# Attention results kept transposed through the out-projection of a hybrid encoder layer

## The chip, the cores and the metric

The kernel runs on one core of a Trainium2 chip. Its engines work side by side, each through a queue of its own in order: TensorE (PE, the matrix multiplier; PEld is its weight load), VectorE (DVE), ScalarE (ACT), GpSimd (POOL) and SyncE (SP), which issues nearly all DMAs. The metric is the device time of one execution in microseconds; lower is better.

## What is computed

One encoder layer on x of 1024 tokens by 1024 features, float32, cut here to what the change touches:

```python
hn = rms_norm(x, norm1_g); proj = hn @ w_in          # qa ka va | qb kb vb
out_a = global_gqa_attention(qa, ka, va)             # dense softmax, 8 heads of 64, 2 kv heads
out_b = dilated_mixture_attention(qb, kb, vb)        # 3 dilated windows, 8 heads of 64, merged
mixed = concatenate([rms_norm(out_a, outa_norm_g),   # each over its own 512 features
                     rms_norm(out_b, outb_norm_g)], -1)
x = x + mixed @ w_out
x = x + conv_ffn(rms_norm(x, norm2_g), ...)          # up, depthwise conv, gelu gate, down
```

Each attention result is a sum over keys divided by a softmax denominator; the two RMS norms follow, one scale per token and half.

## The kernel before

The kernel is one stream of Python calls; a scheduler puts each engine's instructions in order from them by its own estimates, and waits are semaphores between the queues. A few instructions are pinned behind another (`tc.issue_after`). Large products run in fp32 split into a high and a low part, three 128x512 matmuls for each product (xh wh, xh wl, xl wh). The stages follow one another: in-projection, dense attention, dilated attention, out-projection, feed-forward.

`qab(t)` is the mix: eight tiles of 128 tokens by 1024 features, the left 512 columns from the dense heads, the right 512 from the dilated ones.

Dense attention has 16 groups g, each one block of 128 queries and one of two kv heads (4 query heads). The scores of eight key tiles come in four pairs (L763, L764), ACT takes the exponential and the high part (L773), DVE the low part (L774), and pv (L747) gathers 66 rows in a PSUM bank: 64 features and the denominator, by 4 x 128 queries. `last` copies the bank to the single buffer F_OT (DVE, L757). One group later `o_turn` has PE transpose it in four pieces (L752), and `o_norm` takes the reciprocal of the denominators (L793) and multiplies it into the mix (L794).

Dilated attention has 8 heads of 4 iterations, n = 4h + i: scores (L976), exponential on ACT (L977), weights from a table on DVE (L985; or L989, L991, L992 for the iterations with a high and a low part), and two iterations later the product with the values (L1004, L1011). After the fourth, ACT copies the two banks to F_OS (L1014, L1015), and `b_out` turns them with eight transposes on PE (L1044), again followed by `o_norm`. Loads of the next heads' keys, values and tables run on SP; POOL prepares some operands.

Out-projection: `mix_sq` sums squares on ACT (L1089), `mix_norm` makes the two scales and brings the right half to the scale of the left (L1098), `mix_tr` transposes four 128x128 pieces on PE (L196) and splits them into high and low (ACT L219, DVE L220). `proj_out` (L1116 to L1118) adds up eight blocks k of 128 features in a pair of banks per tile, out of three pairs. `h2_a` scales the sum and adds x (L1127), then norm2 on ACT and DVE (L1130 to L1140); `h2_b` transposes the result (L196 too) for the up-projection (L1567 to L1569). Weights of w_out are loaded and split (`wo_load`, `wo_high`, `wo_low`) late in the dilated loop.

## Time and profile before

| | |
|---|---|
| median of 3 runs | 1187.44 us (1187.07 to 1187.44) |
| the profiled execution | 1187.63 us, its span 1185.8 us |
| PE busy | 1172.6 us, 99% of the span, 5896 matmuls |
| DVE busy | 1009.8 us, 85% |
| ACT busy | 659.9 us, 56% |
| POOL busy | 332.1 us, 28% |
| DMA on the hardware queue | 146.43 MB, 38.5% of sixteen engines' span |

Busy PE means that some matmul is in flight: matmuls are pipelined and overlap, so what one costs is read from the distance between two starts. A group's idle time names what ended the wait before it. In windows, the numbers in brackets count instructions.

### The profile page before, as it was taken

How to read it: one execution, taken by the hardware profiler on the slowest of the kernel's cores; microseconds unless marked ns; L12 is line 12 of the kernel's file. 1: busy time of each engine (PE TensorE's matmuls, PEld its weight loads, DVE VectorE, ACT ScalarE, POOL GpSimd, SP SyncE). 2: the span in 40 equal slices, each digit the busy share in tenths (PEclk: the TensorE clock that was granted, in tenths of full speed). 3: DMA queues.
4: the chain of work that ended last, by engine and by line, in shares of the span. 5: the costliest groups of instructions: out<-in, count | busy, mean ns of one | idle time of the engine just before them, and what ended most of it. 6: DMA issues, size and time to landing. Idle time of an engine off the chain costs nothing.

```text
span 1185.8 us, 16414 instructions
## 1 busy us (share of the span) xinstructions
PE 1172.6 (99%) x5896; PEld 966.2 (81%) x5896; DVE 1009.8 (85%) x1431; ACT 659.9 (56%) x986; POOL 332.1 (28%) x237
## 2 busy tenths in 40 slices
PE   9999999999999999999999999999999999999998
PEld 8888886666679998887888888888888888888886
DVE  7869888899988887668999999999999997966672
ACT  7865638799887876346534443444534463543431
POOL 0000221510034510011556465555556414000000
PEclk9999999999999999999999999999999999999999
DMA  8556230110036555232223323232323358967961
GB/s 319 179 145 162 80 78 1 25 52 1 10 67 142 127 127 195 72 102 67 81 98 101 112 100 123 80 107 98 116 98 104 114 192 300 333 217 235 313 231 67
DMA packets 122839, 153.30 MB, mean 129 GB/s; under 512 B 51072, under 2 KB 78336, under 8 KB 122624
## 3 DMA queue, kind: packets, MB, share of 16 engines
q1 hardware_dynamic: 120608, 146.43, 38.5%
q0 software_dynamic: 2144, 5.77, 2.2%
q8 instruction: 47, 0.77, 0.3%
q14 instruction: 40, 0.33, 0.1%
HBM read 113.64 MB, written 33.82 MB: 124 GB/s over the span
## 4 chain that ended last, share of the span: by engine, by line
PE 90%; DVE 5%; ACT 2%; POOL 1%; DMA 1%; issue 1%; SPq 0%; ACTq 0%; POOLq 0%; DVEq 0%
PE ps L1569 12%; PE ps L1568 12%; PE ps L1567 12%; PE ps L747 6%; PE ps L1709 6%; PE ps L1711 6%; PE ps L1710 6%; PE ps L439 3%; PE ps L440 3%; PE ps L441 3%; PE ps L976 3%; PE ps L1118 2%; PE ps L1116 2%; PE ps L1011 2%; PE ps L1117 2%; PE ps L763 2%
## 5 line engine op out<-in xcount | busy, mean ns | idle before, releaser
L1567 PE MATMUL ps<-bigr 128*128 128x512 f32 x616 | 239.8, 389 | 0.5 <-ACT bigr L1170 0.5
L1568 PE MATMUL ps<-bigr 128*128 128x512 f32 x616 | 239.7, 389 | 0.0
L1569 PE MATMUL ps<-bigr 128*128 128x512 f32 x616 | 239.6, 389 | 0.0
L1606 DVE SCALAR_TENSOR_TENSOR bigf<-bigf 128x768 f32<-128x768 f32 (+1 forms) x176 | 193.3, 1134 | 0.7
L1535 ACT ACTIVATE bigr<-bigf 128x512 fp32r<-128x512 f32 x154 | 91.7, 622 | 140.9 <-POOL bigf L1527 108.9
L1689 ACT ACTIVATE bigr<-bigf 128x1024 fp32r<-128x1024 f32 (+1 forms) x99 | 83.8, 868 | 115.4 <-PE ps L1711 63.2
L1567 PEld LDWEIGHTS ps<-bigr 128*128 128x128 f32 x616 | 115.6, 188 | 25.0 <-ACT bigr L1170 0.9
L1568 PEld LDWEIGHTS ps<-bigr 128*128 128x128 f32 x616 | 115.6, 188 | 23.9
L1569 PEld LDWEIGHTS ps<-bigr 128*128 128x128 f32 x616 | 115.6, 188 | 23.9
L1690 DVE TENSOR_TENSOR bigr<-bigf,bigr 128x1024 fp32r<-128x1024 f32 (+1 forms) x99 | 97.6, 1005 | 27.5 <-ACT bigr L1689 24.2
L1709 PE MATMUL ps<-bigr 128*128 128x512 f32 x308 | 119.8, 389 | 0.0
L1710 PE MATMUL ps<-bigr 128*128 128x512 f32 x308 | 119.8, 389 | 0.0
L1711 PE MATMUL ps<-bigr 128*128 128x512 f32 x308 | 119.8, 389 | 0.0
L1536 DVE TENSOR_TENSOR bigr<-bigf,bigr 128x512 fp32r<-128x512 f32 x112 | 106.0, 949 | 3.1 <-ACT bigr L1535 2.6
L747 PE MATMUL ps<-bigr 128*66 128x512 f32 x384 | 99.9, 394 | 0.0
L439 PE MATMUL ps<-bigr 128*128 128x512 f32 x224 | 87.4, 390 | 0.0
L441 PE MATMUL ps<-bigr 128*128 128x512 f32 x224 | 87.2, 389 | 0.0
L440 PE MATMUL ps<-bigr 128*128 128x512 f32 x224 | 87.2, 389 | 0.0
L774 DVE TENSOR_TENSOR bigr<-bigf,bigr 128x1024 fp32r<-128x1024 f32 x64 | 81.0, 1271 | 5.3 <-ACT bigr L773 4.8
L1572 DVE TENSOR_TENSOR bigf<-ps,bigf 128x512 f32<-128x512 f32 x110 | 75.0, 681 | 5.1 <-PE ps L1569 4.9
L1536 POOL TENSOR_TENSOR bigr<-bigf,bigr 128x512 fp32r<-128x512 f32 x42 | 66.9, 1593 | 33.0 <-ACT bigr L1535 31.9
L747 PEld LDWEIGHTS ps<-bigr 128*66 128x66 f32 x384 | 50.8, 136 | 29.9
(224 smaller groups left out, 2380.7 us busy)
## 6 DMA issues: line engine op xcount, KB each, us to landing
bigf<-w_down SPq DMA_DIRECT2D x99, 256.0 KB, 4.3
bigf<-w_up SPq DMA_DIRECT2D x44, 512.0 KB, 3.6
bigf<-gscr SPq DMA_DIRECT2D x77, 256.0 KB, 4.4
gscr<-bigf SPq DMA_DIRECT2D x31, 512.0 KB, 2.6
bigf<-x SPq DMA_DIRECT2D x16, 512.0 KB, 4.4
bigf<-w_in SPq DMA_DIRECT2D x29, 256.0 KB, 3.1
bigf<-xT SPq DMA_DIRECT2D x16, 256.0 KB, 6.6
bigf<-w_out SPq DMA_DIRECT2D x8, 512.0 KB, 3.5
```

The source lines that it names most:

```text
L439: mm(o, r(a, 128), r(w, 512), start=(k == 0 and n != 2 and (c == 1 or n != 3)), stop=False, skip_group_check=True)
L440: mm(o, r(a, 128), r(w + 512, 512), start=False, stop=False, skip_group_check=True)
L441: mm(o, r(a + 512, 128), r(w, 512), start=False, stop=(k == 3), skip_group_check=True)
L747: mm(bank(ob)[0:66], r(w, 66), r(p + 512 * u, 512), start=(kt == 0 and i == 0), stop=(kt == 7 and i == 2))
L1536: low = lambda eng: eng.tensor_tensor(rp(o + 512, [128, 4], [1, 128]), src, rfp(o, [128, 4], [1, 128]), op=OP.subtract)
L1567: mm(bank(b), wh, th, start=(k == 0 and n in (1, 5, 6, 7)), stop=False, skip_group_check=True)
L1568: mm(bank(b), wh, tl, start=False, stop=False, skip_group_check=True)
L1569: mm(bank(b), wl, th, start=False, stop=(k == 3), skip_group_check=True)
L1606: vec.scalar_tensor_tensor(f(a + o, n), f(i + d, n), w_, f(a + o, n), op0=OP.mult, op1=OP.add)
L1709: mm(o, ah, r(d, 512), start=(q == 0 and n in (1, 5, 2)), stop=False, skip_group_check=True)
L1710: mm(o, ah, r(d + 1024, 512), start=False, stop=False, skip_group_check=True)
L1711: mm(o, al, r(d, 512), start=False, stop=(q == NQ - 1), skip_group_check=True)
```

## The change

The transposes between attention and out-projection are left out. In the new form the mix holds features on partitions and tokens along the free axis: in tile `qab(t)` block k of 128 columns is feature block k of those 128 tokens, which is what the matmuls take as weights.

Dense: `last` issues four DMAs on SP for each group. Two move the 64 feature rows from F_OT into the mix (L763; `qab(b)`, 64 partitions each), two write the denominators to `dna` in DRAM (L765). After eight groups `recip_load` brings 128x32 denominators to the chip, `recip` takes one reciprocal and stores it to `rna`, and `scale_load` spreads a row of it over 64 partitions by DMA. `scale_a` multiplies the mix by it on DVE; `squares` squares on ACT and adds four feature blocks on DVE (a 128x128 sum), and `squares_sum` adds up the partitions by matmuls with a column of ones (128x1). All this is placed in groups 8 to 15 (`dense_late`) and in the dilated loop for the second half (`dilated_late`).

Dilated: values come three iterations after the scores, not two. After a head's last iteration a DMA gathers the denominators into 128x8; one iteration later `b_move` moves the features into the mix, another one later `b_recip` takes the reciprocal, stores it to `rnb` and spreads it over 64 partitions, and `scale_b` multiplies two heads at once.

Out-projection: each tile's sum comes in two parts, u = 0 (dense half, four k) and u = 1 (dilated half), each with the two halves of 512 columns in banks of its own. `part_add` (L1195) scales a part by its own norm and adds x or the sum so far. The sixteen parts run in the order `parts`; `mix_split` (ACT L1200, DVE L1201) splits what `mix_tr` gave before. The Sqrt of the dense half's norm stands behind the dilated loop in the program. Blocks 4 and 5 of w_out are split after the loop. A general branch of the program, for inputs beyond a limit, keeps the old form and is not run here.

```diff
-            def o_turn():
-                t = next_tr()
-                for i in range(4):
-                    nc.tensor.transpose(bank(t, 66, 128 * i), f(F_OT + 128 * i, 128)[0:66], f(O_IDF, 66)[0:66])
-                o_norm(t, 128, qab(b) + 256 * kv, ([64, 4], [1, 64]))
-
             def last():
                 pv(3)
                 vec.tensor_copy(f(F_OT, 512)[0:66], bank(ob)[0:66])
+                for u in range(2):
+                    dma(f(qab(b) + 256 * kv, 256)[64 * u:64 * u + 64].rearrange("p (c n) -> p c n", c=2),
+                        fp(F_OT + 128 * u, [256, 2], [1, 128])[0:64])
+                    dma(dna[u:u + 1, b, 256 * kv:256 * kv + 256].rearrange("o (c n) -> o c n", c=2),
+                        fp(F_OT + 128 * u, [256, 2], [1, 128])[64:65])
 
...
-            behind, turn[:] = turn[:], [o_turn]
-            return [lambda: [t() for t in [lambda: pv(1)] + behind], lambda: pv(2), last, o_turn if g == 15 else None]
+            return [lambda: pv(1), lambda: pv(2), last]
+
+        def recip_load(half):
+            dma(fp(F_RC + 32 * half, [16, 2], [1, 16]), dna[:, 4 * half:4 * half + 4, :].rearrange("u b (p e) -> (b p) u e", e=16))
+
+        def recip(half):
+            vec.reciprocal(f(F_RC + 32 * half, 32), f(F_RC + 32 * half, 32))
+            dma(rna[:, 4 * half:4 * half + 4, :].rearrange("u b (p e) -> (b p) u e", e=16), fp(F_RC + 32 * half, [16, 2], [1, 16]))
+
+        def spread_row(dst, row, n):
+            return bass.AP(tensor=row.tensor, offset=row.offset, ap=[[0, 64], [1, n]])
+
+        def scale_load(t):
+            for u in range(2):
+                dma(rf(R_RBA[t % 3], 512)[64 * u:64 * u + 64], spread_row(None, rna[u, t], 512))
+
+        def scale_a(t):
+            vec.tensor_tensor(f(qab(t), 512), f(qab(t), 512), rf(R_RBA[t % 3], 512), op=OP.mult)
+
+        def squares(t, half, where, n):
+            act(f(F_SQ[where], 512), f(qab(t) + 512 * half, 512), AF.Square)
+            vec.tensor_reduce(f(F_ACS[where] + 128 * (n % 2), 128), fp(F_SQ[where], [1, 128], [128, 4]), axis=AX.X, op=OP.add)
+
+        def squares_sum(ns, where, dst):
+            b = next_tr()
+            for c, n in enumerate(ns):
+                mm(bank(b, 1, c), f(F_ACS[where] + 128 * (n % 2), 128), f(O_ONE, 1), start=True, stop=True)
+            if where == 2:
+                vec.tensor_scalar(f(dst + ns[0], len(ns)), bank(b, len(ns)), 1.0 / 512, EPS, op0=OP.mult, op1=OP.add)
+            else:
+                act(f(dst + ns[0], len(ns)), bank(b, len(ns)), AF.Copy, scale=1.0 / 512, bias=EPS)
 
```
```diff
             if i == 3:
                 act(f(F_OS, 512)[0:65], bank(6)[0:65], AF.Copy)
                 act(f(F_OS + 512, 512)[0:65], bank(7)[0:65], AF.Copy)
+                rec = f(F_RC + 64 + 8 * (h % 2), 8)
+                dma(rec, f(F_OS, 1024)[64:65].rearrange("o (p e) -> o p e", e=8))
+
+        def b_move(h):
+            p = 64 * (h % 2)
+            for hf in range(2):
+                dma(fp(qab(hf) + 512 + 128 * (h // 2), [2048, 4], [1, 128])[p:p + 64], heads(f(F_OS + 512 * hf, 512)[0:64], 4))
+
+        def b_recip(h):
+            p, o = 64 * (h % 2), F_RC + 64 + 8 * (h % 2)
+            vec.reciprocal(f(o, 8), f(o, 8))
+            dma(rnb[h].rearrange("(p e) -> p e", e=8), f(o, 8))
+            dma(rf(R_RBB[h // 2 % 2], 1024)[p:p + 64], spread_row(None, rnb[h], 1024))
+
+        def scale_b(m):
+            o = fp(qab(0) + 512 + 128 * m, [1024, 2], [2048, 4], [1, 128])
+            vec.tensor_tensor(o, o, rfp(R_RBB[m % 2], [512, 2], [128, 4], [1, 128]), op=OP.mult)
 
...
+        def part_bank(i, u, hf):
+            return (0, 1, 2, 3, 6, 7)[(2 * parts.index((i, u)) + hf) % 6]
+
+        def part_out(i, u, hf):
+            b, ks = part_bank(i, u, hf), ((0, 1, 3, 2), (4, 5, 6, 7))[u]
+            for k in ks:
+                xh = r(xs(i) + 128 * k, 128)
+                xl = r(xs(i) + 1024 + 128 * k, 128)
+                wh = r(R_WO[k] + 512 * hf, 512)
+                wl = r(R_WO[k] + 1024 + 512 * hf, 512)
+                mm(bank(b), xh, wh, start=(k == ks[0]), stop=False)
+                mm(bank(b), xh, wl, start=False, stop=False)
+                mm(bank(b), xl, wh, start=False, stop=(k == ks[3]))
+
+        def part_add(i, u):
+            x0, o = F_XS[i % 4], (F_XS[i % 4], qab(seq(i)))[u]
+            scale = f((SM_A + 16 + seq(i), SM_B + i)[u], 1)
+            for hf in range(2):
+                vec.scalar_tensor_tensor(f(o + 512 * hf, 512), bank(part_bank(i, u, hf)), scale, f(x0 + 512 * hf, 512),
+                                         op0=OP.mult, op1=OP.add)
+
+        def mix_split(i, u):
+            src, o = f(qab(seq(i)) + 512 * u, 512), xs(i) + 512 * u
+            act(r(o, 512), src, AF.Copy)
+            vec.tensor_tensor(r(o + 1024, 512), src, rf(o, 512), op=OP.subtract)
+
+        def x_part(i):
+            dma(f(F_XS[i % 4], 1024), perm_rows(x, seq(i), D))
+
+        def scale_out(i, n):
+            v, rt, t = [f(SM_T + o + i, n) for o in (32, 40, 72)]
+            act(rt, v, AF.Sqrt)
+            newton(f(SM_B + i, n), v, rt, t)
```
```diff
+        SM_A, SM_B = SM_T, SM_T + 64
+        dense_late = {8: [(recip_load, 0)], 9: [(recip, 0), (scale_load, 0), (scale_load, 1), (scale_load, 2)],
+                      11: [(scale_a, 0), (squares, 0, 0, 0, 0), (scale_load, 3)],
+                      12: [(scale_a, 1), (squares, 1, 0, 0, 1)],
+                      13: [(scale_a, 2), (squares_sum, (0, 1), 0, SM_A), (squares, 2, 0, 0, 2)],
+                      14: [(scale_a, 3), (squares, 3, 0, 0, 3)], 15: [(squares_sum, (2, 3), 0, SM_A)]}
...
-                h1, i1 = divmod(n - 6, 4)
+                h1, i1 = divmod(n - 8, 4)
                 if h1 >= 0 and i1 == 0:
-                    b_out(h1, 0)
-                    b_out(h1, 1)
-                h1, i1 = divmod(n - 2, 4)
-                if 0 <= n - 2 < 32:
+                    b_recip(h1)
+                if n == 33:
+                    wo_load(5)
+                h1, i1 = divmod(n - 7, 4)
+                if h1 >= 0 and i1 == 0:
+                    b_move(h1)
+                h1, i1 = divmod(n - 3, 4)
+                if 0 <= n - 3 < 32:
                     b_pv_bounded(h1, i1)
                     if i1 == 3 and h1 < 6:
                         load_vc(h1 + 2)
+                if n > 31 and n < 34:
...
                 if n == 32:
-                    act(f(SM_T + 96, 1), bank(3, 1), AF.Sqrt, scale=0.0)
+                    act(f(SM_A + 8, 8), f(SM_A, 8), AF.Sqrt)
+                    newton(f(SM_A + 16, 8), f(SM_A, 8), f(SM_A + 8, 8), f(SM_A + 24, 8))
+
+        dilated_late = {4: [(recip_load, 1)], 5: [(recip, 1), (scale_load, 4), (scale_load, 5), (scale_load, 6)], 9: [(scale_a, 4)],
+                        11: [(squares, 4, 0, 1, 4), (scale_a, 5), (scale_load, 7)], 13: [(squares, 5, 0, 1, 5), (scale_a, 6)],
+                        15: [(scale_b, 0)], 16: [(squares_sum, (4, 5), 1, SM_A)], 17: [(squares, 6, 0, 1, 6), (scale_a, 7)],
+                        19: [(squares, 7, 0, 1, 7)], 22: [(squares_sum, (6, 7), 1, SM_A)], 23: [(scale_b, 1)], 31: [(scale_b, 2)]}
```
```diff
+        def project():
+            for i in range(2):
+                x_part(i)
+            part_out(1, 0, 0)
+            part_out(1, 0, 1)
+            b_move(7)
+            b_recip(7)
+            mix_split(2, 0)
+            mix_split(3, 0)
+            for k in (4, 5):
                 wo_high(k, f(F_PD[3], 1))
                 wo_low(k)
...
+            dma(f(F_G2, 1024), bcast(norm2_g, 1024))
+            part_add(0, 0)
+            part_out(2, 0, 0)
+            part_out(2, 0, 1)
+            scale_b(3)
+            for i in range(2):
+                mix_split(i, 1)
+                squares(seq(i), 1, 2, i)
+            for k in (6, 7):
+                wo_high(k)
+                wo_low(k)
+            part_add(1, 0)
+            x_part(2)
+            x_part(3)
+            squares_sum((0, 1), 2, SM_T + 32)
+            scale_out(0, 2)
+            for n in range(3, 16):
...
+                part_out(i, u, 0)
+                apart = parts[n - 1] != (i - 1, 1)
+                if apart:
+                    for t in turn:
+                        h2_b(t, 0)
+                part_out(i, u, 1)
+                if not apart:
+                    for t in turn:
+                        h2_b(t, 0)
+                for t in turn:
+                    h2_b(t, 1)
+                if n == 3:
+                    part_add(2, 0)
+                if u:
+                    h2_a(i)
+                    if i < 4:
+                        x_part(i + 4)
+                    if i == 0:
+                        wu_load(0)
+                else:
+                    part_add(i, 0)
+                if 3 < i + 1 < 8 and not u:
+                    mix_split(i + 1, 0)
+                if u and 0 < i < 7:
+                    mix_split(i + 1, 1)
+                    squares(seq(i + 1), 1, 2, i + 1)
+                    squares_sum((i + 1,), 2, SM_T + 32)
+                    scale_out(i + 1, 1)
```

`parts` is (0,0), (1,0), (2,0), (3,0), (0,1), (1,1), (4,0), (2,1), (5,0), (3,1), (6,0), (4,1), (7,0), (5,1), (6,1), (7,1), written as (tile, u).

How the order moves, at three places. First PE in the dilated loop, in the last heads, before (L976, L1011 and L1004 are scores and values; L1044 the head's turn, L196 a turn of the mix):

```order
L1004 MATMUL ps<-bigr 66x4x48 x3
L196 MATMUL ps<-bigf 128x128 x4
L976 MATMUL ps<-bigr 128x256 x8
L1011 MATMUL ps<-bigf 65x128 x8
L976 MATMUL ps<-bigr 128x256 x8
L1044 MATMUL ps<-bigf 128x65 x8
L1004 MATMUL ps<-bigr 66x4x48 x3
```

and after (L1014, L1049 and L1042 are those three groups):

```order
L1014 MATMUL ps<-bigr 128x256 x8
L1049 MATMUL ps<-bigf 65x128 x8
L1014 MATMUL ps<-bigr 128x256 x8
L1042 MATMUL ps<-bigr 66x4x48 x3
L1042 MATMUL ps<-bigr 66x4x64 x6
L1042 MATMUL ps<-bigr 66x4x48 x3
L1042 MATMUL ps<-bigr 66x4x16 x3
```

Scores and values follow each other with nothing between them. On DVE at a head's end, before:

```order
L985 TENSOR_TENSOR bigf<-ps,bigf 128x1024
L793 RECIPROCAL bigf<-ps 128x4
L794 TENSOR_TENSOR bigf<-ps,bigf 128x4x64
L793 RECIPROCAL bigf<-ps 128x4
L989 TENSOR_TENSOR bigf<-ps,bigf 128x1024
L794 TENSOR_TENSOR bigf<-ps,bigf 128x4x64
L991 CAST bigr<-bigf 128x1024
```

and after (L1023 was L985; L1027, L1029 and L1030 were L989, L991 and L992):

```order
L1030 TENSOR_TENSOR bigr<-bigf,bigr 128x1024
L1023 TENSOR_TENSOR bigf<-ps,bigf 128x1024
L818 TENSOR_REDUCE bigf<-bigf 128x128
L1064 RECIPROCAL bigf<-bigf 128x8
L1027 TENSOR_TENSOR bigf<-ps,bigf 128x1024
L1029 CAST bigr<-bigf 128x1024
L1030 TENSOR_TENSOR bigr<-bigf,bigr 128x1024
```

The four instructions of o_norm are gone; one reciprocal L1064 of b_recip stands behind the weights of the iteration with i = 3, and a reduce L818 of the dense half beside it.

Second, DVE where the out-projection begins, before (o_norm of the last head, then mix_norm, with the Newton steps L207 to L210):

```order
L793 RECIPROCAL bigf<-ps 128x4
L794 TENSOR_TENSOR bigf<-ps,bigf 128x4x64
L1094 TENSOR_SCALAR bigf<-bigf 128x2 x2
L207 RECIPROCAL bigf<-bigf 128x2
L208 TENSOR_TENSOR bigf<-bigf 128x2
L209 SCALAR_TENSOR_TENSOR bigf<-bigf 128x2
L210 SCALAR_TENSOR_TENSOR bigf<-bigf 128x2
L1097 SCALAR_TENSOR_TENSOR bigf<-bigf 128x1
L207 RECIPROCAL bigf<-bigf 128x2
L1098 TENSOR_SCALAR bigf<-bigf 128x512
```

and after (L1195 part_add, L1126 low parts of w_out, L1070 scale_b(3), L1201 mix_split, L818 squares):

```order
L1195 SCALAR_TENSOR_TENSOR bigf<-ps,bigf 128x512
L1064 RECIPROCAL bigf<-bigf 128x8
L1195 SCALAR_TENSOR_TENSOR bigf<-ps,bigf 128x512
L1126 SCALAR_TENSOR_TENSOR bigr<-bigf,bigr 128x1024 x2
L1195 SCALAR_TENSOR_TENSOR bigf<-ps,bigf 128x512 x5
L1070 TENSOR_TENSOR bigf<-bigf,bigr 128x2x4x128
L1201 TENSOR_TENSOR bigr<-bigf,bigr 128x512
L818 TENSOR_REDUCE bigf<-bigf 128x128
L1201 TENSOR_TENSOR bigr<-bigf,bigr 128x512
L1195 SCALAR_TENSOR_TENSOR bigf<-ps,bigf 128x512
```

The last scaling of the mix stands behind the additions of the first three tiles and half of the fourth, and the splits that the parts with u = 1 need stand behind it.

Third, SP's queue in the dense stage after, from the DMAs of group 2 to those of group 3, with what each row waits for (before, the loads L857, L843 and L840 were L819, L805 and L802, with no DMA of a result between them):

```order
L763 DMA bigf<-bigf 64x2x128 [waits DVE_49,DMAHW5_49,Activation_49,Pool_49]
L765 DMA dna<-bigf 2x1x128 [waits DMAHW6_49]
L763 DMA bigf<-bigf 64x2x128 [waits DMAHW7_49]
L765 DMA dna<-bigf 2x1x128 [waits DMAHW0_49]
L857 DMA bigf<-tee 128x384 [waits DMAHW1_49,Pool_49]
L843 DMA bigf<-vscr 128x8x64 [waits DMAHW2_49]
L840 DMA bigf<-kscr 128x8x64 [waits DMAHW3_49,DVE_49]
L763 DMA bigf<-bigf 64x2x128 [waits DMAHW4_49,DVE_49,Activation_49]
L765 DMA dna<-bigf 2x1x128 [waits DMAHW5_49]
L763 DMA bigf<-bigf 64x2x128 [waits DMAHW6_49]
L765 DMA dna<-bigf 2x1x128 [waits DMAHW7_49]
```

The moves of group 3 stand behind loads for the dilated stage, the first of which waits for POOL.

146 lines of the change are left out of this document (90 added, 56 removed).

## The prediction

> **What bounds the kernel now.** I read the page first (span, slices, chain), then the waits of the tensor engine, then busy time by stage, then single stretches of the timeline.
>
> ```profile
> span 1185.8 us, 16414 instructions
> PE   9999999999999999999999999999999999999998
> PE 90%; DVE 5%; ACT 2%; POOL 1%; DMA 1%; issue 1%; SPq 0%; ACTq 0%; POOLq 0%; DVEq 0%
> ```
>
> TensorE (PE) is busy in every slice and carries 90% of the chain that ended last. The profiled execution took 1187.63 us (1185.8 of span and 1.8 around it), 0.19 us above the median of 1187.44; the sum below goes against 1187.63. What PE waits for is small, and three rows of its waits matter here:
>
> ```profile
> PE ps L196 <- DVE bigf L1140: 1.7, 1, 1.7
> ...
> PE ps L752 <- DVE bigf L757: 0.9, 1, 0.9
> ...
> PE ps L1567 <- ACT bigr L1170: 0.5, 1, 0.5
> ```
>
> The change works in four stages: dense attention (186 to 341 us), dilated attention (to 455), out-projection (to 548) and the transition to the feed-forward part.
>
> ```profile
> 186.00:341.00 155.00, 152.74 (x744) 105.23 (x743) 141.74 (x212) 133.91 (x162) 28.53 (x31) 1.00 0.09 20
> 341.00:455.00 114.00, 113.64 (x1010) 108.29 (x1009) 97.11 (x121) 84.81 (x127) 40.34 (x35) 1.00 0.58 139
> 455.00:548.00 93.00, 93.00 (x463) 76.68 (x462) 60.55 (x155) 45.84 (x106) 9.03 (x7) 1.00 0.32 105
> 548.00:600.00 52.00, 49.81 (x223) 40.64 (x223) 48.19 (x70) 27.69 (x43) 22.29 (x15) 1.00 0.21 67
> ```
>
> The columns are length, then busy time of PE, weight loads, DVE, ACT and POOL, the granted clock, the DMA share and GB/s. PE is the limit in all four, at full clock; DVE has 13 us free in the dense stage, 17 in the dilated one, 32 in the out-projection and 4 behind it. So a PE instruction that goes is worth its whole issue time, and what the change lays on DVE, on SP's queue and on DMA latency costs only where it eats that room up.
>
> **PE work that goes.** Matmuls overlap, so I take distances from start to start, not busy times. In the dense stage one turn of a group's result (L752, four 66x66 transposes) reads:
>
> ```profile
> 266.05 0.41 PE L752 MATMUL ps<-bigf 66*128 66x66 f32 x4
> 266.26 0.48 PE L763 MATMUL ps<-bigr 128*128 128x512 f32 x1
> 266.58 0.39 PE L764 MATMUL ps<-bigr 128*128 128x512 f32 x1
> 266.81 0.39 PE L763 MATMUL ps<-bigr 128*128 128x512 f32 x1
> ```
>
> The transposes hold PE for 0.21 us, and the matmul behind them is followed after 0.32 instead of 0.23 us. So a turn costs 0.30 us, sixteen of them 4.8 us, and the 0.9 us that PE waited for L757 goes with them. In the dilated stage a head's eight transposes (L1044):
>
> ```profile
> 376.82 0.84 PE L1044 MATMUL ps<-bigf 65*128 65x65 f32 x8
> 377.47 1.58 PE L1004 MATMUL ps<-bigr 128*66 128x192 f32 x15
> 379.25 1.18 PE L976 MATMUL ps<-bigr 128*128 128x256 f32 x8
> ...
> 385.05 1.18 PE L976 MATMUL ps<-bigr 128*128 128x256 f32 x8
> ...
> 389.13 0.83 PE L1044 MATMUL ps<-bigf 65*128 65x65 f32 x8
> ```
>
> 0.65 us a head, eight heads: 5.2 us; a head lasts 389.13 - 376.82 = 12.3 us. In the out-projection a turn of the mix (mix_tr, L196, four 128x128):
>
> ```profile
> 467.86 0.60 PE L196 MATMUL ps<-bigf 128*128 128x128 f32 x4
> 468.22 0.48 PE L1116 MATMUL ps<-bigr 128*128 128x512 f32 x1
> 468.53 0.39 PE L1117 MATMUL ps<-bigr 128*128 128x512 f32 x1
> ```
>
> That is 0.36 plus 0.31 - 0.23 = 0.44 us. Of the 128 transposes of L196 (row below) half are the mix's, the others are norm2's and stay: 16 x 0.44 = 7.0 us. Together 17.0 us of issue time and 0.9 us of wait leave PE.
>
> **PE work that comes.** The sums of squares now need a sum over partitions: sixteen 128x1 matmuls (squares_sum), in eleven places. The trace has none such. Their weights are 128x128 fp32, as the operands of a transpose are, so the nearest row is L196: 0.09 us each and 0.08 for each change of kind, 1.4 + 0.9, about 2.3 us. Below, the price could fall to 1 us (the changes of kind and little else); above, eleven times a whole turn, 4.8 us. The matmuls of the out-projection stay the same in number; they only come in sixteen parts of 24 over six PSUM banks.
>
> **DVE, dense and dilated.** Rows of what goes or serves as a price:
>
> ```profile
> L504 DVE TENSOR_REDUCE bigf<-bigf 128x16 f32<-128x1024 f32 x12 | 14.4, 1217 | 4.5 <-ACT bigf L501 4.5
> L196 PE MATMUL ps<-bigf 128*128 128x128 f32 x128 | 18.4, 273 | 1.7 <-DVE bigf L1140 1.7
> L794 DVE TENSOR_TENSOR bigf<-ps,bigf 128x256 f32<-128x256 f32 x32 | 13.4, 422 | 1.1
> L1127 DVE SCALAR_TENSOR_TENSOR bigf<-ps,bigf 128x512 f32<-128x512 f32 x16 | 12.0, 750 | 13.4 <-PE ps L1118 13.2
> L793 DVE RECIPROCAL bigf<-ps 128x4 f32<-128x4 f32 x32 | 5.5, 175 | 3.2 <-PE ps L752 2.3 <-PE ps L1044 0.8
> L1098 DVE TENSOR_SCALAR bigf<-bigf 128x512 f32<-128x512 f32 x8 | 3.9, 486 | 0.2
> ```
>
> Each o_norm (0.18 + 0.42 us) goes: 32 of them, 16 in each attention stage, 9.5 us a stage. Dense gains one reciprocal, four multiplies (scale_a) and four reduces (squares), each about 0.6 by half of L504's 1.22 (bounds 0.42, L794's, and 0.75, L1127's): 5.0 us, so DVE has 4.5 us less in all. These stand in groups 9 to 15, where DVE has least room; there the balance of one group is about +1 us against PE, which the order has three score steps to absorb. I cost that at nothing; if the cover were gone it would be 1 us. The reciprocal of the first half waits for its load of the denominators, behind the stores of group 7; what DVE has queued ahead of it lasts about as long, so a wait of up to 1 us is in that same cover. The dilated stage gains four scale_a and four reduces (4.8), three scale_b of 128x1024 (1.2 each, by L504's size) and nine small reciprocals (1.6): 10.0 us against 9.5, a draw.
>
> **Waits on DMA.** 124 DMAs are added, all on SP: four per dense group (64), two loads and two stores of denominators, sixteen spreads of them, and per dilated head one gather of the denominators, two moves, one store and one spread. POOL's queue gets none. Landing times of the rows nearest in kind:
>
> ```profile
> bigf<-x SPq DMA_DIRECT2D x16, 512.0 KB, 4.4
> bigr<-bigr POOLq DMA_DIRECT2D x16, 256.0 KB, 3.5
> gscr<-bigf SPq DMA_DIRECT2D x11, 256.0 KB, 2.0
> kvscr<-bigf SPq DMA_DIRECT2D x8, 128.0 KB, 6.1
> ```
>
> So a small store or gather takes 2.0 to 6.1 us; I take 2.5, nearer the fast end because the pieces move 4 KB, and 4.4 for the last spread, which goes out beside loads of x. In the dilated loop b_recip(h) makes DVE wait for the gather of head h, and behind it in DVE's queue stand the probabilities that PE needs. The copies that start the gather (L1014, L1015) end one iteration later than before, and the reciprocal stands between L985 and L989 of the iteration after that. The same place in the trace before:
>
> ```profile
> 376.07 0.59 ACT L1015 ACTIVATE bigf<-ps 65x512 f32<-65x512 f32 x1
> ```
> ```profile
> 381.57 1.22 DVE L985 TENSOR_TENSOR bigf<-ps,bigf 128x1024 f32<-128x1024 f32 x1
> 384.62 1.22 DVE L989 TENSOR_TENSOR bigf<-ps,bigf 128x1024 f32<-128x1024 f32 x1 [1.83 <-ACT ps L977]
> ```
>
> The copy ends at 376.66; one iteration (12.3 / 4 = 3.1 us) later is 379.74, and DVE comes to the reciprocal at 382.79, 3.0 us behind. DVE then idles 1.83 us anyway, and the scores that need L985's bank start at 385.05, 2.26 us after it. A gather of 2.5 us costs nothing; one of 6.1 us would use up 3.1 of the 4.1 us of room. Cost: 0.
>
> The Sqrt of the dense half's norm now runs inside the dilated loop, on ACT between exponentials:
>
> ```profile
> L1450 ACT ACT_TABLE_LOAD x1 | 1.3, 1283 | 0.0
> ```
>
> Two loads there (Sqrt and back to Exp) hold ACT 2.6 us, against the 2.26 of room: between 0 and 2.6 us, I take 0.7, what is over it and a little of what ACT has behind it.
>
> **Out-projection.** DVE gains a second addition per half tile (16 x 0.75 = 12.0), eight reduces (4.9), the last scale_b (1.2) and the split of one more block of weights (1.2), and loses mix_norm's scaling (3.9) and the last head's two o_norm (1.2): 60.6 becomes about 75 in about 85 us. The new chain starts when the last head's result is done (0): copies 1.2, gather 2.5, reciprocal 0.2, store 2.5, spread 4.4 give 10.8 us. Meanwhile PE runs parts (1,0), (2,0), (3,0), 24 x 0.228 = 5.5 us each, and comes to part (0,1) at 16.4. DVE's queue has scale_b(3) behind the addition of the first half of (3,0): 13.7 + 0.75 = 14.4. So the queue and not the DMAs sets it; scaled at 15.6, split on ACT at 16.3 and on DVE at 17.0: 0 to 0.6 us of stall, 0.5 taken. At the end the additions of the last tiles, their norm and L1140 stand closer together on a fuller DVE, where it already has 48 of 52 us: the wait of 1.7 us on L1140 grows by my estimate to 2.5, with 0 to 1.5 before each of the two tiles ahead of it, taken as 0.6 each: +2.0. From below the 1.7 could vanish; from above 8 us if every tile from the third on waits 1 us more.
>
> **The sum.** 1187.63 - 4.8 - 5.2 - 7.0 - 0.9 + 2.3 + 0.7 + 0.5 + 2.0 = 1175.2, less the 0.19 to the median: 1175.0.
>
> **Rivals.**
> Full gain: the table loads and both out-projection stalls stay hidden and the 128x1 matmuls cost 1 us: 1187.4 - 17.9 + 1.2 = 1170.7. For it speaks the 17 to 32 us of free DVE time; against it the existing 1.7 at the end.
> DVE becomes the bound in the out-projection: additions, reduces, splits, norms and transposed copies run in one queue, and banks come free only by the additions. If each of the eight tiles costs 1 us instead of my 2.5 us in all, 1180.5; the upper end is 1185. It begins when DVE's 75 us come near 85, at a tenth more than I counted.
> Small pieces: gather and store move 32-byte pieces, and both take kvscr's 6.1 us. Then the last chain is 1.2 + 6.1 + 0.2 + 6.1 + 4.4 = 18.0 instead of 14.4, a stall of 3.6 us more: 1178.6; the dilated loop still hides its own. Against it: the packets of the fast rows land in 2.0. [...]
> [...]
> Other side: SP's queue holds the dense results. F_OT is one buffer; its next copy on DVE must wait for all four DMAs out of it, and they stand in SP's queue between loads that wait for POOL.
>
> ```profile
> 227.29 0.11 POOL L1434 MEMSET bigf<- 128x8 f32 x1
> ...
> 245.07 1.68 POOL L829 TENSOR_TENSOR bigr<-bigf,bigr 128x512 fp32r<-128x512 f32 x1 [4.84 <-ACT bigr L828]
> ```
> ```profile
> 234.25 0.68 DVE L757 COPY bigf<-ps 66x512 f32<-66x512 f32 x1
> ```
>
> The first such load comes free at 227.29, 7 us before group 3 is copied. The next waits for POOL's work that ends at 246.75, with group 4's DMAs behind it, while group 5 is copied at about 254 (two groups of 155 / 16 = 9.7 after 234.25): they need some 4 us (the landing of 2.5 and four issues), so 3 are left. Every us of a later release costs PE one, through DVE; from 15 us later on (3 + the 12.4 gained) the kernel is slower, and at 18 us later it takes 1190.4. POOL would have to be that late for another reason, since its own work is untouched.
> That the turns stay in the program is excluded: the order has no L752, L1044 or mix_tr left on the path taken.
>
> **Chances and range.** The forecast (1172.5 to 1178.5) 0.46; full gain 0.17; DVE bound 0.20, 0.03 of it past 1185.07; small pieces 0.06; SP's queue 0.07; a mixture that ends near no change 0.04. A measurement tells 0.2% (2.4 us) from nothing: faster 0.46 + 0.17 + 0.17 + 0.06 = 0.86, same 0.07, slower 0.07. From 1169.5 to 1184 leaves out 0.02 below and 0.16 above.
>
> **What would show it.** No L752 and L1044 rows and 64 fewer L196; dense stage about 5 us shorter, dilated 4 to 5, out-projection 4 to 5; a DVE wait on DMA at the reciprocals without a PE wait behind it; in PE's waits one on the split of part (0,1) under 1 us and one on L1140's successor of 2 to 3 us. A dense stage that isn't shorter, with DVE's F_OT copy waiting for DMA, would make it wrong, as would PE waits on the additions in most parts.

## The result and the profile after

| | before | after |
|---|---|---|
| median | 1187.44 us (1187.07 to 1188.74, 4 runs) | 1196.72 us (1194.66 to 1197.74, 4 runs) |
| profiled execution, its span | 1187.63, 1185.8 us | 1197.74, 1196.0 us |
| PE busy, matmuls | 1172.6 us, 5896 | 1169.5 us, 5736 |
| DVE busy | 1009.8 us | 1018.8 us |
| mean granted clock | 0.999 | 0.994 |

The ratio is 1.0074, interval 1.0057 to 1.0091: the changed kernel is 0.7% slower, 9.3 us, where the forecast was 12.4 us faster. From the page after, the span and the chain that ended last:

```profile
span 1196.0 us, 16295 instructions
...
PE 77%; DVE 7%; DMA 6%; ACT 4%; issue 3%; POOL 2%; SPq 1%; DVEq 0%; POOLq 0%; ACTq 0%
```

PE has less to do, and its share of the chain fell from 90% to 77%; DMA went from 1% to 6%. The waits of PE, after:

```profile
PE ps L1187 <- ACT bigr L1200: 3.6, 1, 3.6
PE ps L1014 <- DVE bigf L1023: 3.5, 1, 3.5
PE ps L772 <- DVE bigf L463: 2.5, 2, 1.6
PE ps L206 <- DVE bigf L1233: 2.5, 4, 1.1
PE ps L1042 <- ACT bigf L1052: 1.7, 2, 1.1
```

Two single waits of 3.5 and 3.6 us are new, one in the dilated loop (L1014, scores) and one in the out-projection (L1187). The two stages in the windows of before (length; busy PE, weight loads, DVE, ACT, POOL; clock; DMA share; GB/s):

```profile
341.00:455.00 114.00, 108.01 (x914) 102.86 (x912) 92.25 (x100) 85.36 (x129) 39.93 (x36) 0.96 0.70 168
455.00:548.00 93.00, 88.94 (x422) 72.97 (x420) 67.25 (x144) 36.57 (x73) 5.17 (x4) 0.98 0.41 121
```

The clock fell from 1.00 to 0.96 and 0.98, and the DMA share rose from 0.58 to 0.70 and from 0.32 to 0.41.

Where the time went is seen by following the same matmul in two traces. The table has its start before, and how much later it starts in the changed kernel and in the last version of the experiments (all mends, second schedule); numbers count from 0:

| matmul | before, us | after | all mends 2 |
|---|---|---|---|
| 100th of the program | 18.02 | +2.2 | +0.0 |
| dilated scores, iteration 0 | 343.78 | +1.1 | -3.0 |
| iteration 10 | 375.80 | -1.7 | -6.0 |
| iteration 13 | 385.05 | +6.3 | -6.4 |
| iteration 31 | 439.65 | +4.6 | -5.8 |
| out-projection, 56th of L1187 and L1189 (before: L1116 and L1118) | 468.22 | +3.5 | -7.1 |
| 72nd | 475.07 | +7.8 | -4.5 |
| 240th | 541.38 | +6.5 | -5.9 |
| up-projection, 44th of L1687 (before: L1567) | 581.40 | +10.2 | -2.9 |

The first 2.2 us aren't the change's: the instructions there are the same, and in three of the ten experiments the 100th matmul was 1.8 to 2.1 us late too, in the others 0.0 to 0.4. The large losses beside it have four places: 1.6 us at the start of the dense stage, 8.0 between iterations 10 and 13, 4.3 between the 56th and the 72nd matmul of the out-projection, 3.7 at its end; between them time is mostly gained.

**The 8.0 us.** SP's queue in the dilated loop, after (start, length, line, transfers):

```profile
364.91 0.38 SPq L804 DMA_DIRECT2D rna<-bigf  x1
365.38 0.50 SPq L849 DMA_DIRECT2D bigf<-vscr  x1
365.98 0.83 SPq L843 DMA_DIRECT2D bigf<-vscr  x1
369.08 3.70 SPq L811 DMA_DIRECT2D bigr<-rna  x6
372.88 0.54 SPq L1055 DMA_DIRECT2D bigf<-bigf  x1
```

The dense half's reciprocals are stored (L804); the first of the six spreads (L811) waits for that store, and all six are issued one after the other at 0.6 us each. Behind them stands the gather of head 0's denominators (L1055). Its source had been complete since 365.72 (the end of ACT's second copy, 365.14 + 0.58); it was issued 7.2 us later. On DVE and PE, after:

```profile
372.52 1.23 DVE L1030 TENSOR_TENSOR bigr<-bigf,bigr 128x1024 fp32r<-128x1024 f32 x1
379.41 0.20 DVE L1064 RECIPROCAL bigf<-bigf 128x8 f32<-128x8 f32 x1 [5.67 <-DMA bigf<-bigf]
379.53 1.19 DVE L1023 TENSOR_TENSOR bigf<-ps,bigf 128x1024 f32<-128x1024 f32 x1
```
```profile
376.75 0.54 PE L203 MATMUL ps<-bigr 128*128 128x128 f32 x4
380.77 2.08 PE L1014 MATMUL ps<-bigr 128*128 128x256 f32 x8 [3.48 <-DVE bigf L1023]
```
```profile
370.00:380.00 10.00, 7.29 (x70) 7.15 (x68) 3.73 (x5) 3.06 (x5) 2.36 (x3) 0.97 0.84 179
380.00:390.00 10.00, 8.13 (x42) 7.84 (x43) 7.51 (x9) 7.41 (x12) 3.55 (x2) 0.51 0.53 137
```

The reciprocal of eight columns waits 5.67 us for a transfer of 4 KB, with the weights of the next scores (L1023) behind it; PE waits 3.48 us for these, and comes back at a granted clock of 0.51: eight score matmuls take 2.08 us instead of 1.18.

**The 4.3 us.** SP and DVE where the out-projection begins, after:

```profile
459.17 0.53 SPq L1055 DMA_DIRECT2D bigf<-bigf  x1
...
461.08 0.65 SPq L1204 DMA_DIRECT2D bigf<-x  x1
...
465.33 0.57 SPq L1065 DMA_DIRECT2D rnb<-bigf  x1
466.36 0.33 SPq L1912 DMA_DIRECT2D bigf<-norm_g  x1
467.15 0.33 SPq L1204 DMA_DIRECT2D bigf<-x  x1
467.53 0.49 SPq L1066 DMA_DIRECT2D bigr<-rnb  x1
```
```profile
463.54 0.21 DVE L1120 CAST bigr<-bigf 128x1 fp32r<-128x1 f32 x2 [6.02 <-DMA bigf<-x]
...
474.42 0.75 DVE L1195 SCALAR_TENSOR_TENSOR bigf<-ps,bigf 128x512 f32<-128x512 f32 x1 [4.26 <-DMA bigf<-x]
476.24 1.23 DVE L1070 TENSOR_TENSOR bigf<-bigf,bigr 128x1024 f32<-128x1024 f32 x1 [1.07 <-DMA bigr<-rnb]
```

From the gather's issue (459.17) to the scaling that needs the spread (L1070, 476.24) it is 17.1 us. The last spread (256 KB) alone takes 476.24 - 467.53 = 8.7 us, with 512 KB loads of norm2's weights and of x right ahead of it in the queue. DVE also waits by itself for x, first with L1120, which is tied to a place that the loads of x write.

### The profile page after: what moved, and what is told of

Read it like the earlier page. It is cut to its first block, busy times and chain, and to the rows that moved or that the text cites. A ratio compares the mean times of both kernels' runs of the same rounds, so it can differ in the third digit from the quotient of the medians.

```text
span 1196.0 us, 16295 instructions
## 1 busy us (share of the span) xinstructions
PE 1169.5 (98%) x5736; PEld 961.7 (80%) x5736; DVE 1018.8 (85%) x1402; ACT 659.5 (55%) x975; POOL 332.0 (28%) x238
## 4 chain that ended last, share of the span: by engine, by line
PE 77%; DVE 7%; DMA 6%; ACT 4%; issue 3%; POOL 2%; SPq 1%; DVEq 0%; POOLq 0%; ACTq 0%
PE ps L1689 11%; PE ps L1687 11%; PE ps L1688 11%; PE ps L1829 6%; PE ps L1830 6%; PE ps L1831 6%; PE ps L757 6%; PE ps L450 2%; PE ps L449 2%; PE ps L451 2%; PE ps L772 2%; PE ps L773 2%; PE ps L1187 2%; PE ps L1189 2%; PE ps L1188 1%
## 5 line engine op out<-in xcount | busy, mean ns | idle before, releaser
L1687 PE MATMUL ps<-bigr 128*128 128x512 f32 x616 | 240.0, 390 | 0.6 <-ACT bigr L1263 0.5
L1687 PEld LDWEIGHTS ps<-bigr 128*128 128x128 f32 x616 | 115.6, 188 | 25.9 <-ACT bigr L1263 1.0
L757 PE MATMUL ps<-bigr 128*66 128x512 f32 x384 | 99.8, 394 | 0.6 <-DVE bigr L783 0.6
L757 PEld LDWEIGHTS ps<-bigr 128*66 128x66 f32 x384 | 51.1, 136 | 31.5 <-DVE bigr L783 1.1
```

The lines of the kernel that those rows point to most:

```text
L757: mm(bank(ob)[0:66], r(w, 66), r(p + 512 * u, 512), start=(kt == 0 and i == 0), stop=(kt == 7 and i == 2))
L1687: mm(bank(b), wh, th, start=(k == 0 and n in (1, 5, 6, 7)), stop=False, skip_group_check=True)
```

## The experiments

The theory: two new transfers stand on the path, and SP's queue and the loads ahead of them, not their own size, make them late. Rivals: the DMA traffic as such; DVE as the bound; turns on PE that cost less than I took. The runs are in the order in which they were made; each is compared with runs of the kernel before on the same chip.

**Another queue for the gather.**

```diff
-                dma(rec, f(F_OS, 1024)[64:65].rearrange("o (p e) -> o p e", e=8))
+                nc.scalar.dma_start(rec, f(F_OS, 1024)[64:65].rearrange("o (p e) -> o p e", e=8))
```

> Only the gather of each head's denominators (b_pv_bounded) is issued on ScalarE's queue, right behind the copies it depends on, instead of SP's. Theory A (SP's queue in order: head 0's gather stood behind six spreads of 0.6 us each and their wait for a store, from 365.7 to 372.9 us, DVE then waited 5.7, PE 3.5 + 1.1, and the clock fell to half for some 9 us; 8.0 us lost between scores 10 and 13): the gather lands before 370, the wait and the half clock go, about 1196.7 - 8 = 1188.7 us; 1187 to 1190 with 0.3 us per issue on ScalarE. Theory B (the transfers themselves are slow, 6.5 us from issue to landing, because the spreads fill the DMA engines): issued at 366 the gather still lands near 372, DVE waits about 2 us, no half clock, 1190 to 1192. Theory C (DVE is simply too full in the dilated loop): no change, 1194 to 1198.

Measured: 1197.57 us (1197.12 to 1198.88), ratio 1.0083 [1.0066, 1.0100]. The first event is gone, as theory A had it: the gather goes out at 366.14, the reciprocal starts at 369.46 without a wait, and iteration 13 is 1.1 us earlier than before. The first three gathers took 0.56, 0.48 and 0.48 us to issue on ACT's queue; the 0.3 us per issue in the expectation is shown by no run. But the time is not the 1188.7 of that theory: it was lost again in two later places. PE's waits in this run:

```profile
PE ps L1187 <- ACT bigr L1200: 5.2, 1, 5.2
PE ps L1042 <- ACT bigf L1052: 3.9, 3, 2.5
```

The 5.2 are in the out-projection, where DVE waits 4.7 us for the last spread. The 3.9 are in three waits; the longest (2.5 at 406.73, in the dilated loop) stands behind a square on ACT that waits 2.3 us for scale_a on DVE. So the queue order explains the first event; of the two later ones one is a late spread again, the other a wait between ACT and DVE and no transfer.

**The spreads later.** The six spreads are no longer issued together at iteration 5, ahead of the gather; one multiply (scale_a of tile 4) moves one iteration later with them.

```diff
-5: [(recip, 1), (scale_load, 4), (scale_load, 5), (scale_load, 6)], 9: [(scale_a, 4)],
+5: [(recip, 1)], 8: [(scale_load, 4)], 9: [(scale_load, 5)], 10: [(scale_a, 4)], 12: [(scale_load, 6)],
```

> The gather stays on SP; the spreads of the dense half's second part are taken out of its way: scale_load of tiles 4, 5 and 6 in iterations 8, 9 and 12 instead of all in iteration 5, scale_a(4) in 10 instead of 9. Theory A: the same gain as with the gather on ScalarE, 1187 to 1190 us, and the gather of head 0 issued at about 366. Theory B: also the gain, since the traffic is gone too. Theory C: 1194 to 1198. If this gains and the gather on ScalarE doesn't, it is traffic; if both gain, it is the queue.

Measured: 1190.49 us (1189.34 to 1191.94, 10 runs), ratio 1.0017 [1.0007, 1.0027]: 6.2 us of the 9.3. The gather is now issued ahead of the spreads:

```profile
369.93 1.40 SPq L1055 DMA_DIRECT2D bigf<-bigf  x1
...
374.88 1.14 SPq L811 DMA_DIRECT2D bigr<-rna  x2
```

Its reciprocal starts at 373.65 without a wait, and between iterations 10 and 13 the trace gains 0.3 us where it lost 8.0. Between the 56th and 72nd matmul of the out-projection it loses only 0.2 us instead of 4.3. A wait of 2.3 us (L1042 on ACT's copy) stands at 408.5, behind a square on ACT that waits for scale_a on DVE; from iteration 13 to 31 this trace loses 2.9 us where the changed kernel gained 1.7. So the 6.2 us are a balance, and the gain in the out-projection did not come again in the later run with the same places for the spreads (later spreads and fills). The largest single step of the loss is still the place of six spreads in one queue.

**Order in the out-projection.** The loads of x behind b_recip(7) in the program, the splits of w_out's blocks 4 and 5 ahead of them, norm_g last, and the first part_add held behind the reciprocal.

```diff
-            for i in range(2):
-                x_part(i)
             part_out(1, 0, 0)
             part_out(1, 0, 1)
             b_move(7)
             b_recip(7)
+            for i in range(2):
+                x_part(i)
...
```

> Only project() is written in another order: the splits of blocks 4 and 5 of w_out ahead of the loads of x (their tie reads the place where x of tile 0 is loaded, and DVE waited 6.0 us for it), b_move(7) and b_recip(7) ahead of x, part_add(0,0) held behind that reciprocal, the load of norm2_g after scale_b(3) in the program. Theory A (the last head's denominators are late because DVE, in order, waits for x ahead of the reciprocal, and SP issues x and norm2_g ahead of the spread): the reciprocal comes 2 to 3 us earlier, the stall of 3.6 us before part (0,1) and the lower clock behind it (drift from +3.5 to +7.8 in the profile, 4.3 us) go at least by half: 1192 to 1194.5 us. Theory B (the DMA chain itself takes that long, with 8.7 us for the spread): same, 1195.5 to 1198.

Measured: 1197.25 us (1196.02 to 1199.43), ratio 1.0073 [1.0057, 1.0090]: the gain of theory A did not come, the time is that of theory B. The scheduler didn't follow the program's order: on SP norm_g (454.34), x (456.26), w_up (457.46) and x (457.89) went ahead of the gather (458.96), which landed 8.7 us later.

```profile
PE ps L823 <- DVE bigf L818: 5.1, 1, 5.1
```

The stall stayed and only changed its name. In this run a 4 KB transfer took 8.7 us behind 512 KB loads.

**Turns twice, in the kernel before.** Every turn of dense, dilated and mix results is done twice (eight transposes for four).

```diff
-                for i in range(4):
+                for i in (0, 1, 2, 3, 0, 1, 2, 3):
...
```

> The kernel before, with every transpose of o_turn, b_out and mix_tr done twice into the same place: nothing else added. It measures the term of 17.0 us. If the issue times of the timeline hold (0.21 x 16 + 0.65 x 8 + 0.36 x 16 = 14.3 us without the changes of kind), 1201.7 us, 1199 to 1204.5 with the waits that a later result brings. If the transposes were largely hidden (the forecast's term wrong), under 1194.

Measured: 1201.52 us (1200.8 to 1202.31), ratio 1.0111 [1.0094, 1.0128], 13.5 us above the kernel before (1188.02 there). The prices of the transposes on PE hold; the rival that turns are nearly free falls.

**Loads behind gather and spread.** As the third experiment wanted, now pinned: x(0), x(1) behind the gather; norm_g, x(2), x(3) and w_up behind the last spread.

```diff
+            with tc.issue_after(probs[0]):
+                for i in range(2):
+                    x_part(i)
...
+            with tc.issue_after(spread7):
+                dma(f(F_G2, 1024), bcast(norm2_g, 1024))
...
```

> project() again, but now for the traffic and not only the order on DVE: the loads of x for tiles 0 and 1 are issued behind the last head's gather, and those of norm2_g, x for tiles 2 and 3 and w_up behind the spread of its denominators; the ties ahead of x as before, part_add(0,0) behind the reciprocal. In the run with only another order the gather, a DMA of 4 KB, landed 8.7 us after its issue, behind 512 KB loads of norm2_g, x and w_up. Theory B (the DMA engines take transfers in the order of issue, so a small one waits for the big ones ahead): the gather lands within 3 us, the reciprocal comes about 4 us earlier, the stall before part (0,1) goes, and with it the lower clock behind it: 1196.7 - 4 = 1192.5 us, 1191 to 1194. Theory A (queue order on DVE and SP alone): no better than the last, 1195.5 to 1198, the gather still late.

Measured: 1195.19 us (1193.69 to 1196.96), ratio 1.0058 [1.0043, 1.0072]. Between the 56th and 72nd matmul the trace loses 1.3 us instead of 4.3. The median is 1.5 us below the changed kernel's, and the two ratios' intervals overlap: the gain is seen in the trace, not yet in the times. The first half of theory B came true: the gather, issued at 458.89 with no 512 KB load right ahead of it, landed in 2.1 us (the reciprocal that waits for it starts at 460.97, and at 464.33 in the changed kernel). The stall did not go with it. DVE's waits in that stretch:

```profile
DVE bigf L1195 <- DMA bigf<-x: 4.7, 2, 3.8
DVE bigf L1070 <- DMA bigr<-rnb: 3.5, 1, 3.5
```

The spread still comes 3.5 us late: the store ahead of it was issued at 462.67 and the spread, which waits for it, at 468.28. This time the two loads of x stood ahead of the store.

**The fills back in their groups.** Four scalings of another operand (`fills`, L1274) had lost their tie to a group in the change, by the constant O_IDF, and the scheduler put them ahead of the dense stage. On DVE, after:

```profile
190.35 1.62 DVE L1274 TENSOR_SCALAR bigr<-bigf 64x512 fp32r<-64x512 f32 x3
192.01 0.69 DVE L463 TENSOR_TENSOR bigf<-ps,bigf 128x512 f32<-128x512 f32 x1
```

PE waits for that L463 (the row L772 of PE's waits above, 2.5 us).

```diff
-                fills.pop(0)(O_IDF if bounded else qab(b) + 256 * kv)
+                fills.pop(0)(F_PB[g % 3] if bounded else qab(b) + 256 * kv)
```

> Only the tie of the four fills (64x512 on DVE) is changed: to the probabilities that were written last, not to a constant. In the changed kernel they stand all four at the start of the dense stage, ahead of an addition of the in-projection for which PE waits; before, they stood one each in later groups. If that is what delays the start of the dense stage (PE's wait for that addition 2.5 instead of 0.9 us), 1.6 us go: 1195 us, 1193.5 to 1196. If the delay came from something else in that place, 1196 to 1197.5 and the wait stays 2.5.

Measured: 1192.95 us (1191.95 to 1199.17, 6 runs), ratio 1.0037 [1.0025, 1.0050]: 3.8 us below the changed kernel. The wait on L463 falls from 2.5 to 0.9, which is 1.6 of it; the profiled execution of this kernel was its longest run (1199.17), so its trace can't show the other 2.2. The other traces show a part. From the first dense scores of group 0 to those of group 1 the changed kernel's trace loses 1.8 us against before, but those of the five experiments on it that leave the fills ahead (another queue, later spreads, order, loads, short spreads) lose 2.7 to 3.0: in each of them PE's clock is half for 3.4 us right behind that wait, and in the trace after it isn't. The four with the fills back lose nothing there (-0.1 to 0.0).

**All mends.** The last two and a schedule of my own for the dilated loop (spreads at 8, 9, 12, 16; squares and their sums later too).

```diff
+        dilated_late = {4: [(recip_load, 1)], 5: [(recip, 1)], 8: [(scale_load, 4)], 9: [(scale_load, 5)], 12: [(scale_load, 6), (scale_a, 4)],
+                        13: [(scale_a, 5)], 14: [(squares, 4, 0, 1, 4)], 15: [(scale_b, 0)], 16: [(scale_load, 7), (squares, 5, 0, 1, 5)],
+                        17: [(squares_sum, (4, 5), 1, SM_A), (scale_a, 6)], 19: [(squares, 6, 0, 1, 6)], 21: [(scale_a, 7)],
...
```

> All mends together: the fills, the loads behind the last gather and spread, and in the dilated loop the spreads of tiles 4 and 5 at iterations 8 and 9, of 6 and 7 at 12 and 16, with each multiply and square two or more iterations behind what it waits for. If the losses add up (6.2 measured for the spreads, 1.6 for the fills, about 4 for the end of the dilated loop): 1196.7 - 12 = 1185 us, 1182 to 1188, about the kernel before or a little faster. If they are one and the same backlog that only moves on, 1188 to 1192. If the forecast's 17 us of PE time were all to come through, 1176; I don't expect that, since the dense stage gave 3 instead of 5.7 us even where nothing waits for a DMA.

Measured: 1188.23 us (1186.01 to 1190.98, 12 runs), ratio 0.9997 [0.9988, 1.0005]. The time is that of the second case expected, a loss that moves on. Of the changed kernel's four losses three are gone or small in the trace (dense start 0.0, iterations 10 to 13 -0.3, out-projection 0.9); the one at the end of the out-projection stays (3.6). And squares_sum at iteration 17 waits 2.5 us for a sum that the same DVE queue makes only then, and 3.5 us are lost there.

**Short spreads.** Queue order against traffic, for the six spreads:

```diff
+            n = 8 if t > 3 else 512
-                dma(rf(R_RBA[t % 3], 512)[64 * u:64 * u + 64], spread_row(None, rna[u, t], 512))
+                dma(rf(R_RBA[t % 3], n)[64 * u:64 * u + 64], spread_row(None, rna[u, t], n))
```

> The spreads of tiles 4 to 7 in the dilated loop move 8 of their 512 columns; number and order of all transfers stay as in the changed kernel. What is left out: the other columns of those spread denominators (their values are then old ones). Queue-order theory: the six spreads still take 0.6 us each on SyncE's queue behind the wait for the stored reciprocals, head 0's gather is still issued near 372.9 us, VectorE still waits for it, and the loss between scores 10 and 13 (8.0 us) stays in full: 1196 to 1197.5. Traffic theory: the gather, though issued late, lands about 2.5 us later instead of 6.5, the wait on VectorE shrinks from 5.7 to under 2, TensorE does not idle for 3.5 us, its clock does not halve, and most of the 8.0 goes: 1189 to 1191. Both half: the wait falls by the 4 us of the landing, TensorE still idles 1 to 2 us but keeps its clock: 1190 to 1193.

Measured: 1201.79 us (1200.35 to 1203.0), ratio 1.011 [1.0096, 1.0125]. SP and DVE in this run (L812, L1056 and L1065 are L811, L1055 and L1064 here):

```profile
367.89 3.70 SPq L812 DMA_DIRECT2D bigr<-rna  x6
371.69 0.54 SPq L1056 DMA_DIRECT2D bigf<-bigf  x1
```
```profile
377.01 0.20 DVE L1065 RECIPROCAL bigf<-bigf 128x8 f32<-128x8 f32 x1 [6.52 <-DMA bigf<-bigf]
```

Six spreads of 2 KB take the queue for the same 3.70 us as six of 128 KB, and while they went out the engines were nearly idle (DMA share and GB/s in the last columns):

```profile
368.00:370.00 2.00, 2.00 (x22) 2.00 (x20) 1.86 (x2) 1.01 (x1) 0.00 (x0) 1.00 0.05 7
370.00:372.00 2.00, 2.00 (x21) 2.00 (x20) 0.49 (x1) 1.74 (x3) 0.84 (x2) 1.00 0.06 3
```

The wait stayed (6.5 us), and 8.9 us were lost between iterations 10 and 13. So the bytes of the spreads are not the cause, their places in the queue are. The traffic theory's other half fell too: the gather took 5.3 us with the spreads' bytes away, 6.5 with them (the moves go out right behind it, at 372.33; no run took these away). The total is 4 us above the range of the queue-order theory and 11 above that of the traffic theory; part of it is a longer stall in the out-projection (PE's wait on L1201, 5.4 us, at a clock of 0.77 from 480 to 490; 6.1 us lost between the 56th and 72nd matmul instead of 4.3), which this edit does not touch.

**Later spreads and fills together** (second and sixth experiment).

> The later spreads (2nd experiment) and the four filling scalings put back in their groups (6th) together, out-projection left as changed. If the losses add up as separate events, the time is that of the 2nd experiment less what the fills cost in their own run: 1190.5 - 3.8 = 1186.7, faster than before by about 0.1%. If what the fills win is lost again at the first place that waits on a transfer, as in the run with all mends together, it comes out at 1189 to 1190.5.

Measured: 1188.2 us (1185.47 to 1191.52, 12 runs), ratio 1.0002 [0.9991, 1.0014], between the two figures. In its trace the out-projection stalls again (3.6 us between the 56th and 72nd matmul, a wait of 2.9 on L1200), where the second experiment alone had lost 0.2. Its loads of x are those of the changed kernel; DVE's first wait for them (L1120) was 6.9 us here and 5.2 in the second experiment, and why they came later here is not shown.

**All mends, second schedule.** The squares stay where the change had them where they can, only spreads and scalings move (the other edits are those of all mends):

```diff
+        dilated_late = {4: [(recip_load, 1)], 5: [(recip, 1)], 8: [(scale_load, 4)], 9: [(scale_load, 5)], 10: [(scale_a, 4)],
+                        11: [(squares, 4, 0, 1, 4), (scale_a, 5)], 12: [(scale_load, 6)], 13: [(squares, 5, 0, 1, 5)], 14: [(scale_a, 6)],
+                        15: [(scale_b, 0), (scale_load, 7)], 16: [(squares_sum, (4, 5), 1, SM_A)], 17: [(squares, 6, 0, 1, 6)], 19: [(scale_a, 7)],
+                        20: [(squares, 7, 0, 1, 7)], 23: [(squares_sum, (6, 7), 1, SM_A), (scale_b, 1)], 31: [(scale_b, 2)]}
...
```

> Like the run of all mends together (out-projection's loads behind the gather and the spread, fills back, spreads later), but the dilated loop's schedule keeps the squares at their old iterations and only the spreads and the scalings are moved, so that the new wait at scores 16 to 18 (3.5 us: sum of squares behind VectorE) should go. If it goes: 1188.2 - 3.5 = 1184.7, faster than before by 0.3%. If the out-projection's loads behind the gather merely move their cost to the end of the stage, where VectorE is the bound: 1187 to 1188.5.

Measured: 1182.95 us (1181.99 to 1184.97, 6 runs), ratio 0.9957 [0.9945, 0.9968]: 0.43% faster than the kernel before, and 13.8 us below the changed kernel by the medians. Its longest waits of PE:

```profile
PE ps L206 <- DVE bigf L1233: 2.5, 4, 1.1
PE ps L823 <- DVE bigf L818: 1.7, 1, 1.7
PE ps L1014 <- DVE bigf L1027: 1.6, 2, 1.5
```

No single wait above 1.7 us is left. The idea of the change pays; the places of a few DMAs and of four scalings had turned it into a loss. It does not pay what was forecast: 5.4 of 12.4 us. In this trace 3.0 us are won up to the first dilated scores where 5.7 were forecast, 2.6 are lost between the 56th and 72nd matmul of the out-projection instead of 0.5, and 2.9 at its end instead of 2.0. That is 5.7 of the 7.0 us missing; the rest is not settled.

## Why the prediction was wrong

**The step that failed** is the one headed "Waits on DMA": "A gather of 2.5 us costs nothing; one of 6.1 us would use up 3.1 of the 4.1 us of room. Cost: 0." It counted the gather from the end of the copy that feeds it, with a landing time alone. It left out the queue. The gather went out 7.2 us after the copy and took 6.5 more, 13.7 us against 4.1 of room, and a reciprocal of 0.2 us held up the scores. The 124 new DMAs had been counted, and that all stood on SP, but not what stands ahead of this one there: a wait for a store, then six issues of 0.6 us. The second and the short-spread experiment show this: with the spreads moved the 8.0 us at that place were gone (6.2 in the time), with the spreads shrunk 8.9 were lost there. The rival "SP's queue holds the dense results" had the mechanism, at another place: the dense results weren't held, the dilated gather was.

**The out-projection's stall** was taken as 0.5 with the last spread at 4.4 us. The spread took 8.7, and the chain from the gather 17.1 instead of 9.6. "So the queue and not the DMAs sets it" is wrong: DVE stood idle for transfers. The rival of small pieces gave 16.8 us for the same chain, so its size was right, but not its reason. The store of 32-byte pieces, issued at 465.33, had landed when the spread that waits for it was issued at 467.53, 2.2 us later; the same store took 5.6 us in the fifth experiment, behind two loads of x.

**Not seen at all**: the fills. The tie was in the diff and I read it as a detail; the sixth experiment, which put it back, is 3.8 us faster by the medians, and at the start of the dense stage the traces show 1.8 to 3.0 of it. I read DVE's order only in the loop and the out-projection, not where the dense stage begins.

**The clock.** The sum had no term for a lower clock. It came: 0.51 over ten microseconds. In the trace after PE waited 3.48 us up to 380.77 and 3.63 us up to 478.19; the granted clock was half from 379.46 to 389.70 and from 478.45 to 481.86, that is for 10.24 and 3.41 us. A shorter wait was followed by a half clock too. PE in the out-projection, all mends with the second schedule:

```profile
465.46 0.38 PE L823 MATMUL ps<-bigf 128*128 128x1 f32 x2 [1.72 <-DVE bigf L818]
465.70 0.74 PE L1189 MATMUL ps<-bigr 128*128 128x512 f32 x1
466.24 0.63 PE L1187 MATMUL ps<-bigr 128*128 128x512 f32 x1
466.67 0.63 PE L1188 MATMUL ps<-bigr 128*128 128x512 f32 x1
```

and at the same place in the fifth experiment:

```profile
475.81 0.38 PE L823 MATMUL ps<-bigf 128*128 128x1 f32 x2 [1.96 <-DVE bigf L818]
476.06 0.48 PE L1189 MATMUL ps<-bigr 128*128 128x512 f32 x1
476.37 0.40 PE L1187 MATMUL ps<-bigr 128*128 128x512 f32 x1
476.60 0.40 PE L1188 MATMUL ps<-bigr 128*128 128x512 f32 x1
```

After 1.72 us of wait the matmuls start every 0.43 us (466.24 to 466.67), at a granted clock of 0.50 from 466 to 468, up to 469; after the longer wait of 1.96 every 0.23, at a clock of 1.00 from 470 to 480. So the length alone does not decide; what does is not shown.

**What held.** PE's prices: the dense products (L757) of groups 1 to 4 started 3.98, 3.69, 3.38 and 3.10 us later than before, 0.3 less with each group, as taken; doubling all turns cost 13.5 us where 14.3 were expected. The rows of L752 and L1044 are gone, DVE's additions wait less for PE in the out-projection (8.6 us instead of 13.2), and over that stage as a whole DVE is not the bound (67.3 of 93 us busy).

**Smaller misses.** The 128x1 matmuls come as 32 rows, two for each, mostly 0.11 us from one start to the next: with the changes of kind about 3.2 us instead of 2.3. A reduce of the squares (L818) takes 1.08 us on DVE, not 0.6 and outside the bounds of 0.42 and 0.75; over sixteen of them that is 7.6 us more DVE time than counted. The end of the out-projection costs 3.7 us instead of 2.0, with four waits on L1233 (2.5 us) in place of one of 1.7, while DVE is busy for all ten microseconds from 560 to 570. This stayed in all mended versions (2.9 in the last) and was not taken apart; that DVE is the limit there is argued from its busy time, not shown.

**The balance.** Against the forecast the profiled execution is 22.5 us off (1197.74 against 1175.2). 8.0 are the dilated wait with its half clock, 3.8 the out-projection, 1.6 the dense start, 2.2 the program's start, 1.7 the end, 0.9 the small matmuls: 18.2. The other 4 are spread over the dense stage's last groups (1.2) and the dilated loop behind iteration 13; what waits for what there was not settled in single steps.

## What to carry to other kernels

A new DMA on the path is priced from the moment its source is ready to its landing (here 7.2 us up to the issue and 6.5 from there), with all that stands ahead of it in its queue: the waits of those transfers, their issues, and large loads ahead of it (a gather of 4 KB took 2.1 us without and 8.7 behind loads of 512 KB). An instruction of 0.2 us that waits for it costs what stands behind it in its own in-order queue, here 8.0 us between iterations 10 and 13, the half clock included. Where a scheduler sets the order, a changed tie is a change of its own: read the order on each engine at every stage's start, not only around the new code. A wait of the matrix engine is not priced by its length alone: one of 1.72 us was followed here by a granted clock of 0.50, one of 1.96 by one of 1.00, and no run shows what decides.
